# SBUF laid out anew: split weights between the two groups of moving operands, work tiles on the right

## The chip, the cores and the metric

One core of a Trainium2 chip runs the kernel. The metric is the device time of one execution in microseconds (us); lower is better. The program is the same in every execution, so times of three runs and one profiled execution stand for it.

## What is computed

One decoder layer on x of 1024 x 1024 float32: a pooling mixer and a gated convolutional feed-forward network, each behind a root-mean-square norm and with a residual.

```
h = rms_norm(x, norm_mix_g)
# four groups of 256 channels, windows 2, 4, 8, 16:
d = (causal window mean of h) - h
x = x + pool_scale * (d @ pool_w[group] + pool_b)
h = rms_norm(x, norm_ffn_g) @ w_in            # 1024 x 5632
h = causal_depthwise_conv(h, conv_w, conv_b)  # 3 taps
val, gate = split(h)                          # 2816 each
x = x + (silu(gate) * val) @ w_out            # 2816 x 1024
```

## The kernel before, in words

**Stages.** The mixer runs over eight blocks of 128 rows; each block is normed, windowed, multiplied with the pooling weights, added to x (stored to DRAM as x1), normed again and transposed. Then comes the input projection, over 22 pairs of feature blocks (`order`, line 295), and at the end the output projection, over 11 feature pairs.

**Seven products for eight.** Both projections use Strassen's scheme in Winograd's form. A matrix product of 2 x 2 blocks is made of seven block products instead of eight, at the price of sums of blocks. In the input projection the sums of the weights (A11, A12, S1, S2, S3, S4, A22) are made anew for each feature block on VectorE; the sums of the activations (B11, T1, B21, T2, T3, B22, T4) are made once and kept.

**Split operands.** Each operand of a product is split into a high part (float32r, rounded) and a low part, the rest. `split` (line 72) does it for a weight block: ScalarE copies to the high part, VectorE subtracts. `product` (line 339) makes a block product of 12 matmuls of 128x512: for each of four slices of 128 rows, high x high, high x low and low x high. The weights are the stationary operand, the activations (the "nop" tiles) the moving one. In the profile, where numbers at the end of names are left out, "B" stands for B11, B21 and B22 and "T" for T1 to T4; the weight's name beside it tells which, by the table `STEPS`: A11s goes with B11, S2s with T2, S1s with T1, A12s with B21, S3s with T3, S4s with B22, A22s with T4. That is also the order of the products in a round, one round for each n. `event` (line 417) prepares the weights of the product five ahead and issues one product. After it VectorE and ScalarE take the bank's result, and at a round's end `gated` (line 399) makes the convolution, silu and product on VectorE and ScalarE and stores the block to DRAM. X, Y and Z are PSUM banks' tags.

**Output projection.** It loads blocks of the gated activations and of w_out into the nop tiles' places, makes the sums, and splits both operands into "hl" tiles (oAP, oBP), so both the stationary and the moving operand of its matmuls (line 636) are hl tiles.

**Where tiles lie.** SBUF has one address range for each of 128 partitions. Pools are taken from its left end (low addresses) or from its right end (`side="right"`), as stacks. A pool that is closed makes room for the next on its side. Before the change the pools are:

- left, from below: `const`; `nop_a` (B11, T1, B21); `work` (x_edge and later ha; the small sums; the raw weight loads; the seven hl slots; q1); `n2_pool` (n2f, the normed and transposed activations), after it `late` (hb, val, gate, q2), after it `fin` (streams and z);
- right, from the top: `pre` (all of the mixer's setup and blocks), after it `nop_b` (B22, T4, T3, T2) and `right` (r).

In bytes within a partition, as the built programs allocate them:

| tiles | before | after |
|---|---|---|
| B11, T1, B21 (16,384 each) | 17,312 / 33,696 / 50,080 | the same |
| seven hl slots (4,096 each) | 93,088 to 121,760 | 66,464 to 95,136 |
| B22, T4, T3, T2 (16,384 each) | 163,808 / 180,192 / 196,576 / 212,960 to 229,344 | 95,136 / 111,520 / 127,904 / 144,288 to 160,672 |
| r | 159,712 to 163,808 | 160,672 to 164,768 |
| mixer's setup (`pre`) | 159,936 to 229,344 | 95,136 to 164,544 |
| n2f | 125,856 to 158,624 | 165,856 to 198,624 |
| hb, val, gate, q2; later streams and z | 125,856 to 158,624 | 165,856 to 198,624 |
| ha | 66,464 to 70,560 | 198,624 to 202,720 |
| small sums | 70,560 to 76,704 | 202,720 to 208,864 |
| raw weight loads | 76,704 to 93,088 | 208,864 to 225,248 |
| q1 | 121,760 to 125,856 | 225,248 to 229,344 |

In the steady rounds each weight keeps to one hl slot: before, A12s at 93,088, S3s at 97,184, A11s at 101,280, S2s at 105,376, S4s at 109,472, S1s at 113,568, A22s at 117,664; after, the same slots 26,624 lower. Within a nop tile the high part takes the first 8,192 bytes and the low part the rest; each matmul reads 2,048 of them.

Of the kernel before, what the change touches and what calls it, by code (L numbers as in the profile page):

```python
# [7 lines left out]
F32 = mybir.dt.float32  # L8
F32R = mybir.dt.float32r
# [5 lines left out]
P = 128  # L15
S = 1024
D = 1024
F = 2816
NS = S // P
NK = D // P  # L20
# [23 lines left out]
NH = 512  # L44
# [4 lines left out]
def trunk_kernel(ctx: ExitStack, tc: tile.TileContext, x, consts, par, rows, pool_w, w_in, w_out, out):  # L49
# [2 lines left out]
    const = ctx.enter_context(tc.tile_pool(name="const", bufs=1))  # L52
    dram = ctx.enter_context(tc.tile_pool(name="dram", bufs=1, space=bass.MemoryType.DRAM))
    ps_x = ctx.enter_context(tc.tile_pool(name="ps_x", bufs=2, space=PSUM))
    nop_a = ctx.enter_context(tc.tile_pool(name="nop_a", bufs=1))
    work = ctx.enter_context(tc.tile_pool(name="work", bufs=1))
    mid = ExitStack()
    n2_pool = mid.enter_context(tc.tile_pool(name="n2_pool", bufs=1))
    pre = ExitStack()
    pp = pre.enter_context(tc.tile_pool(name="pre", bufs=1, side="right"))  # L60
    ps_p = pre.enter_context(tc.tile_pool(name="ps_p", bufs=3, space=PSUM))

    def bank2(name):
# [3 lines left out]
        return work.tile([P, 2, D], F32, tag="raw", name=name, bufs=2)  # L67

    def hl_tile(name):
        return work.tile([P, 2, NH], F32R, tag="hl", name=name, bufs=7)  # L70

    def split(src, name):
        t = hl_tile(name)
        nc.scalar.activation(t[:, 0, :], src, AF.Copy)  # L74
        nc.vector.tensor_tensor(t[:, 1, :], src, t[:, 0, :].bitcast(F32), ALU.subtract)  # L75
        return t


    xs = {}

    def load_x(j):
        if j < 2 or j >= 2 + XBUFS:
            xs[j] = work.tile([P, D], F32, tag="hl", name=f"x{j}", bufs=7)
        else:
            xs[j] = pp.tile([P, D], F32, tag="x", name=f"x{j}", bufs=XBUFS)
        nc.sync.dma_start(xs[j], x[j * P : (j + 1) * P, :])
# [5 lines left out]
    def affine(t, src, op, fill, base, pattern, step):  # L92
        nc.gpsimd.affine_select(out=t, in_=src, compare_op=op, fill=fill, base=base, pattern=pattern, channel_multiplier=step)
# [26 lines left out]

    keep_warm(12)
    load_x(0)
    nc.sync.dma_start(cst[:, :E0], consts[:, :E0])

    nc.sync.dma_start(x_edge, x.rearrange("(j r) d -> r j d", r=P)[P - HALO :, :, :])
    nc.sync.dma_start(cst[:, E0:], consts[:, E0:])
    load_x(1)
    nc.sync.dma_start(par_sb, par)
    nc.sync.dma_start(scale_b, rows[:1, :].to_broadcast([P, D]))
    for g in range(0, NG, 2):  # L130
        nc.sync.dma_start(wp_raw[:, 2 * g : 2 * g + 4, :], pool_w[g : g + 2].rearrange("g (k p) d -> p (g k) d", p=P))
    for j in range(2, NS):
        load_x(j)
    spread = work.tile([P, NK, P], F32, tag="hl", name="spread", bufs=7)

    eps_t = const.tile([P, 1], F32, tag="eps", name="eps_t")
    nc.vector.memset(eps_t, D * EPS)
# [170 lines left out]
    def tmp(name):  # L308
        return work.tile([P, NH], F32, tag="sum", name=name, bufs=3)
# [30 lines left out]
    def product(bank, a, b, opens):  # L340
        m = 0
        for k in range(4):
            ks = slice(k * P, (k + 1) * P)
            for i, l in ((0, 0), (0, 1), (1, 0)):
                nc.tensor.matmul(bank, a[:, i, ks], b[:, l, k, :], start=opens and m == 0, stop=m == 11, skip_group_check=not opens)  # L345
                m += 1
# [5 lines left out]
    banks, hid = {}, {}  # L352

    def small(tag, name, bufs):
        return work.tile([P, NH], F32, tag=tag, name=name, bufs=bufs)

    def step(n, p):
        a, b, z = STEPS[p]
        opens = p in ("P1", "P6", "P5")
        if opens:  # L360
            pool = ps_x if z == "X" else ps_yz
            banks[n, z] = pool.tile([P, NH], F32, tag=z, name=f"{z}{n}")
        bank = banks[n, z]
        product(bank, aops.pop((n, a)), nops[b], opens)
        tt = nc.vector.tensor_tensor
        if p == "P1":
            hid[n, "q1"] = small("q1", f"q1_{n}", 2)
            nc.scalar.activation(hid[n, "q1"], bank, AF.Copy)
        elif p == "P2":
            hid[n, "a"] = work.tile([P, S], F32, tag="ha", name=f"ha{n}", bufs=1)  # L370
            nc.scalar.activation(hid[n, "a"][:, :NH], bank, AF.Copy)  # L371
        elif p == "P6":
            hid[n, "q2"] = tmp(f"q2_{n}") if n < 2 else late.tile([P, NH], F32, tag="q2", name=f"q2_{n}", bufs=2)
            tt(hid[n, "q2"], bank, hid[n, "q1"], ALU.add)
            if n < 2:
                tt(hid[n, "a"][:, NH:], banks[n, "Z"], hid[n, "q2"], ALU.add)
        elif p == "P5":
            hid[n, "r"] = right.tile([P, NH], F32, tag="r", name=f"r_{n}", bufs=2)
            tt(hid[n, "r"], bank, hid[n, "q1"], ALU.add)
        elif p == "P7":  # L380
            hid[n, "b"] = late.tile([P, S], F32, tag="hb", name=f"hb{n}", bufs=1)
            tt(hid[n, "b"][:, NH:], bank, hid[n, "r"], ALU.add)
        elif p == "P3":
            if n >= 2:
                tt(hid[n, "a"][:, NH:], bank, hid[n, "q2"], ALU.add)  # L385
        else:
            tt(hid[n, "b"][:, :NH], bank, hid[n, "q1"], ALU.add)  # L387
# [29 lines left out]
    def event(k):  # L417
        if k >= 4:
            prep_event(k + LOOK)
        n, p = events[k]  # L420
        step(n, p)
        if p == "P4":
            gated(n)
# [48 lines left out]
            stat(j + 1)  # L472
            stat(j + 2)
    pre.close()
    nop_b = ctx.enter_context(tc.tile_pool(name="nop_b", bufs=1, side="right"))
    right = ctx.enter_context(tc.tile_pool(name="right", bufs=1, side="right"))
    ps_yz = ctx.enter_context(tc.tile_pool(name="ps_yz", bufs=3, space=PSUM))
    for b in ("T2", "T3", "B22", "T4"):
        nops[b] = nop_tile(nop_b, b)
# [22 lines left out]
        split_n(nops["T4"], t4[:, ks], ks=ks)  # L502
    mid.close()
    late_stack = ExitStack()
    late = late_stack.enter_context(tc.tile_pool(name="late", bufs=1))
    for k in range(9, len(events)):
        event(k)
    late_stack.close()


    fin = ctx.enter_context(tc.tile_pool(name="fin", bufs=1))
    free = []

    def take(name):
# [91 lines left out]
    for k in range(-SLOOK, len(oevents)):  # L606
        p, f = oevents[k + SLOOK] if k + SLOOK < len(oevents) else (None, 0)
# [11 lines left out]
        p, f = oevents[k]  # L619
        set_, opens = chains[p]  # L620
        if f == 0 and opens:
            for i in range(4):
                tag = ("XXYY" if set_ == "X" else "YZZZ")[i]
# [92 lines left out]
```

## Time and profile before

| | |
|---|---|
| median of 3 runs | 714.81 us (714.56 to 716.27) |
| the profiled execution's own time | 715.61 us |
| its span, first to last instruction | 713.9 us |
| mean granted TensorE clock | 0.999 |
| matmuls recorded on TensorE | 3149 |

The profile is of one execution. PE is TensorE's matmuls, PEld its weight loads, DVE is VectorE, ACT ScalarE, POOL GpSimd, SP SyncE, which issues the DMAs. A row of the timeline gives the start of a group of equal instructions, the time from its start to its end, its tiles as out<-in, the shape and the count. A matmul's recorded duration holds its way through the array and overlaps the next one, so how long a matmul or a product holds TensorE is read from one start to the next. The chain that ended last is followed back from the last instruction, at each step to what released it. L345 is line 345 of the kernel before; in the kernel after the lines from 55 on are two further down (L347, and L638 for the output projection).

### The profile page before, as it was taken

How to read it: one execution, taken by the hardware profiler on the slowest of the kernel's cores; microseconds unless marked ns; L12 is line 12 of the kernel's file. 1: busy time of each engine (PE TensorE's matmuls, PEld its weight loads, DVE VectorE, ACT ScalarE, POOL GpSimd, SP SyncE). 2: the span in 40 equal slices, each digit the busy share in tenths (PEclk: the TensorE clock that was granted, in tenths of full speed). 3: DMA queues.
4: the chain of work that ended last, by engine and by line, in shares of the span. 5: the costliest groups of instructions: out<-in, count | busy, mean ns of one | idle time of the engine just before them, and what ended most of it. 6: DMA issues, size and time to landing. Idle time of an engine off the chain costs nothing.

```text
span 713.9 us, 8484 instructions
## 1 busy us (share of the span) xinstructions
PE 701.3 (98%) x3149; PEld 572.5 (80%) x3150; DVE 604.8 (85%) x897; ACT 341.9 (48%) x515; POOL 6.5 (1%) x24
## 2 busy tenths in 40 slices
PE   7999999999999999999999999999999999999997
PEld 5898777888888888888888888888887788888885
DVE  4789999999888888888888888876987997798993
ACT  5696546545444544444544444454443544443441
POOL 3000000000000000000000000000000000000000
PEclk9999999999999999999999999999999999999999
DMA  9622032132221122222222212119988800006241
GB/s 307 252 90 87 7 114 75 72 139 80 78 81 53 73 89 89 90 88 90 89 88 89 85 64 89 62 69 350 314 294 295 306 20 1 1 0 206 90 147 59
DMA packets 31001, 83.37 MB, mean 117 GB/s; under 512 B 3416, under 2 KB 4720, under 8 KB 28144
## 3 DMA queue, kind: packets, MB, share of 16 engines
q1 hardware_dynamic: 30864, 82.82, 32.4%
q8 instruction: 24, 0.39, 0.2%
q14 instruction: 17, 0.14, 0.1%
q0 software_dynamic: 96, 0.02, 0.0%
HBM read 62.89 MB, written 19.92 MB: 116 GB/s over the span
## 4 chain that ended last, share of the span: by engine, by line
PE 82%; DMA 8%; DVE 7%; issue 1%; ACT 1%; SPq 1%; POOL 0%; DVEq 0%; ACTq 0%
PE Y L345 24%; PE oP L636 21%; PE X L345 15%; PE Z L345 15%; DMA blk<-g_dram 4%; PE psy L243 3%; DMA blk<-in_w_out_dram 2%; PE psd L172 2%; DVE T L292 1%; DMA x_edge<-in_x_dram 1%; DVE n2f L303 1%; DMA B21s<-in_w_out_dram 1%; PE pst L272 1%; DMA bias_hl<-rows_raw 1%; DVE oBP L75 1%
## 5 line engine op out<-in xcount | busy, mean ns | idle before, releaser
L636 PE MATMUL oP<-oBP,oAP 128*128 128x512 f32 x924 | 211.7, 390 | 1.4 <-DVE oBP L75 0.9
L636 PEld LDWEIGHTS oP<-oBP,oAP 128*128 128x128 f32 x924 | 173.1, 188 | 39.9 <-DVE oBP L75 2.6
L345 PE MATMUL Z<-T,S1s 128*128 128x512 f32 x264 | 65.0, 394 | 1.5 <-ACT T L291 1.1
L345 PE MATMUL X<-B,A11s 128*128 128x512 f32 x264 | 65.6, 394 | 0.7 <-DVE A11s L75 0.7
L345 PE MATMUL Y<-T,S2s 128*128 128x512 f32 x264 | 65.1, 394 | 0.5 <-DVE T L292 0.4
L345 PE MATMUL Y<-T,S3s 128*128 128x512 f32 x264 | 64.3, 392 | 0.0
L345 PE MATMUL Y<-T,A22s 128*128 128x512 f32 x264 | 64.1, 392 | 0.0
L345 PE MATMUL Z<-B,S4s 128*128 128x512 f32 x264 | 63.9, 391 | 0.0
L345 PE MATMUL X<-B,A12s 128*128 128x512 f32 x264 | 63.6, 390 | 0.0
L345 PEld LDWEIGHTS Z<-T,S1s 128*128 128x128 f32 x264 | 49.3, 188 | 13.6 <-ACT T L291 1.6
L345 PEld LDWEIGHTS Y<-T,S2s 128*128 128x128 f32 x264 | 49.3, 188 | 12.5 <-DVE T L292 0.9
L345 PEld LDWEIGHTS X<-B,A11s 128*128 128x128 f32 x264 | 49.3, 188 | 12.2 <-DVE A11s L75 1.1
L345 PEld LDWEIGHTS Y<-T,S3s 128*128 128x128 f32 x264 | 49.5, 188 | 11.2
L345 PEld LDWEIGHTS Y<-T,A22s 128*128 128x128 f32 x264 | 49.5, 188 | 11.1 <-ACT val L392 0.3
L345 PEld LDWEIGHTS Z<-B,S4s 128*128 128x128 f32 x264 | 49.6, 188 | 10.9
L345 PEld LDWEIGHTS X<-B,A12s 128*128 128x128 f32 x264 | 49.5, 188 | 10.3
L403 ACT ACTIVATE gate<-gate 128x1024 f32<-128x1024 f32 x22 | 23.4, 1062 | 43.2 <-DVE gate L394 43.0
L74 ACT ACTIVATE oBP<-blk 128x512 fp32r<-128x512 f32 x32 | 20.2, 633 | 46.9 <-PE oP L636 41.6
L393 DVE SCALAR_TENSOR_TENSOR val<-ha,par_sb,val 128x1023 f32<-128x1023 f32 x22 | 28.2, 1282 | 12.5 <-ACT val L392 12.5
L385 DVE TENSOR_TENSOR ha<-Z,q 128x512 f32<-128x512 f32 x20 | 13.8, 692 | 23.9 <-PE Z L345 23.8
L392 ACT ACTIVATE gate<-hb,par_sb 128x1024 f32<-128x1024 f32 x22 | 27.4, 1245 | 11.9 <-DVE hb L387 11.9
L371 ACT ACTIVATE ha<-X 128x512 f32<-128x512 f32 x22 | 13.2, 600 | 41.2 <-PE X L345 41.2
(129 smaller groups left out, 1020.5 us busy)
## 6 DMA issues: line engine op xcount, KB each, us to landing
win<-in_w_in_dram SPq DMA_DIRECT2D x22, 1024.0 KB, 4.8
g_dram<-val SPq DMA_DIRECT2D x22, 512.0 KB, 2.6
blk<-g_dram SPq DMA_DIRECT2D x33, 256.0 KB, 5.4
blk<-in_w_out_dram SPq DMA_DIRECT2D x31, 256.0 KB, 5.5
A12s<-g_dram SPq DMA_DIRECT2D x22, 256.0 KB, 4.6
B21s<-in_w_out_dram SPq DMA_DIRECT2D x22, 256.0 KB, 2.6
x<-in_x_dram SPq DMA_DIRECT2D x8, 512.0 KB, 9.6
x_dram<-x SPq DMA_DIRECT2D x8, 512.0 KB, 2.6
```

Source lines behind the costliest of these rows:

```text
L74: nc.scalar.activation(t[:, 0, :], src, AF.Copy)
L75: nc.vector.tensor_tensor(t[:, 1, :], src, t[:, 0, :].bitcast(F32), ALU.subtract)
L172: m = nc.tensor.matmul(ps[:, c * P : (c + 1) * P], src[:, c * P : (c + 1) * P], weights[:, c // 2, :], start=True, stop=True)
L243: nc.tensor.matmul(o, dh[:, c, :], wps[:, c, :], start=c % 4 == 0, stop=False, skip_group_check=True)
L272: nc.tensor.transpose(ps[:, c * P : (c + 1) * P], n2[:, c * P : (c + 1) * P], ident)
L345: nc.tensor.matmul(bank, a[:, i, ks], b[:, l, k, :], start=opens and m == 0, stop=m == 11, skip_group_check=not opens)
L371: nc.scalar.activation(hid[n, "a"][:, :NH], bank, AF.Copy)
L385: tt(hid[n, "a"][:, NH:], bank, hid[n, "q2"], ALU.add)
L392: nc.scalar.activation(t, src, AF.Identity, bias=par_sb[:, CB + f : CB + f + 1], scale=w[2])
L393: nc.vector.scalar_tensor_tensor(t[:, 1:], src[:, : S - 1], w[1], t[:, 1:], op0=ALU.mult, op1=ALU.add)
L403: nc.scalar.activation(gate, gate, AF.Silu)
L636: nc.tensor.matmul(obanks[set_, i], a[:, u, i * P : (i + 1) * P], b[:, v, :], start=opens and g == 0 and m == 0, stop=g == NP2 - 1 and m = ...
```

## The change

Some pools change sides and one new pool is made. The hl tiles (split weights, and some x blocks early on) get a pool of their own, `hls`, taken on the left right after `nop_a`. `pre`, and after it `nop_b` and the pool of r, come next on the left. `work`, `n2_pool`, `late` and `fin` go to the right. No instruction is added, removed or moved: each engine has the same instructions in the same order (559 rows of equal instructions on PE, 891 on DVE, 499 on ACT, 16 on POOL, 202 on SP), and each of them waits for the same values of the same semaphores as before. The pool that takes the place of `pre` still waits for it, and the one that takes the place of `n2_pool` for that. What is different in the built program is the addresses in the table above.

```diff
     nop_a = ctx.enter_context(tc.tile_pool(name="nop_a", bufs=1))
-    work = ctx.enter_context(tc.tile_pool(name="work", bufs=1))
+    hls = ctx.enter_context(tc.tile_pool(name="hls", bufs=1))
+    work = ctx.enter_context(tc.tile_pool(name="work", bufs=1, side="right"))
     mid = ExitStack()
-    n2_pool = mid.enter_context(tc.tile_pool(name="n2_pool", bufs=1))
+    n2_pool = mid.enter_context(tc.tile_pool(name="n2_pool", bufs=1, side="right"))
     pre = ExitStack()
-    pp = pre.enter_context(tc.tile_pool(name="pre", bufs=1, side="right"))
+    pp = pre.enter_context(tc.tile_pool(name="pre", bufs=1))
...
     def hl_tile(name):
-        return work.tile([P, 2, NH], F32R, tag="hl", name=name, bufs=7)
+        return hls.tile([P, 2, NH], F32R, tag="hl", name=name, bufs=7)
...
         if j < 2 or j >= 2 + XBUFS:
-            xs[j] = work.tile([P, D], F32, tag="hl", name=f"x{j}", bufs=7)
+            xs[j] = hls.tile([P, D], F32, tag="hl", name=f"x{j}", bufs=7)
...
-    spread = work.tile([P, NK, P], F32, tag="hl", name="spread", bufs=7)
+    spread = hls.tile([P, NK, P], F32, tag="hl", name="spread", bufs=7)
...
         elif p == "P5":
-            hid[n, "r"] = right.tile([P, NH], F32, tag="r", name=f"r_{n}", bufs=2)
+            hid[n, "r"] = left.tile([P, NH], F32, tag="r", name=f"r_{n}", bufs=2)
...
     pre.close()
-    nop_b = ctx.enter_context(tc.tile_pool(name="nop_b", bufs=1, side="right"))
-    right = ctx.enter_context(tc.tile_pool(name="right", bufs=1, side="right"))
+    nop_b = ctx.enter_context(tc.tile_pool(name="nop_b", bufs=1))
+    left = ctx.enter_context(tc.tile_pool(name="left", bufs=1))
...
-    late = late_stack.enter_context(tc.tile_pool(name="late", bufs=1))
+    late = late_stack.enter_context(tc.tile_pool(name="late", bufs=1, side="right"))
...
-    fin = ctx.enter_context(tc.tile_pool(name="fin", bufs=1))
+    fin = ctx.enter_context(tc.tile_pool(name="fin", bufs=1, side="right"))
```

## The prediction

> **What bounds the kernel now.** I read the page first, then busy time by stage, then the timeline of TensorE through one round, then the chain that ended last. On the page TensorE is busy nearly all the time:
>
> ```profile
> PE 701.3 (98%) x3149; PEld 572.5 (80%) x3150; DVE 604.8 (85%) x897; ACT 341.9 (48%) x515; POOL 6.5 (1%) x24
> ```
>
> The stages (columns: stretch, its length, busy time and instructions of TensorE's matmuls, its weight loads, VectorE, ScalarE and GpSimd, then the granted clock, the DMA share and GB/s) tell where TensorE is not the only limit:
>
> ```profile
> 62.00:125.00 63.00, 60.37 (x270) 47.86 (x269) 62.12 (x88) 34.36 (x52) 0.00 (x0) 1.00 0.20 72
> 125.00:490.00 365.00, 365.00 (x1592) 298.55 (x1591) 311.41 (x404) 171.67 (x232) 0.00 (x0) 1.00 0.24 88
> 490.00:560.00 70.00, 68.58 (x296) 54.86 (x295) 58.96 (x91) 32.58 (x53) 0.00 (x0) 1.00 0.93 320
> 560.00:710.00 150.00, 149.50 (x659) 123.25 (x657) 127.68 (x208) 61.03 (x105) 0.00 (x0) 1.00 0.23 80
> ```
>
> Before 125 us VectorE has no slack (62.12 of 63.00). From 125 to 490 us TensorE never stops (365.00 of 365.00) while VectorE has 53.6 us of slack; around 490 to 560 us the DMA engines are 93% busy; the last stretch is TensorE's again. The clock is granted in full in each stage, so a matmul that takes longer than another doesn't do so for its clock.
>
> What a page cannot show is that equal matmuls do not take equal time. Here is one round of the long stage, a feature block of the input projection: seven products of 12 matmuls each, the same instruction with the same shapes. The columns are start, busy time to the end of the last one's pipeline, and the names; the time a product holds TensorE is the next row's start less its own.
>
> ```profile
> 322.84 2.93 PE L345 MATMUL X<-B,A11s 128*128 128x512 f32 x12
> 325.61 2.93 PE L345 MATMUL Y<-T,S2s 128*128 128x512 f32 x12
> 328.38 2.93 PE L345 MATMUL Z<-T,S1s 128*128 128x512 f32 x12
> 331.15 2.88 PE L345 MATMUL X<-B,A12s 128*128 128x512 f32 x12
> 333.87 2.93 PE L345 MATMUL Y<-T,S3s 128*128 128x512 f32 x12
> 336.63 2.91 PE L345 MATMUL Z<-B,S4s 128*128 128x512 f32 x12
> 339.38 2.91 PE L345 MATMUL Y<-T,A22s 128*128 128x512 f32 x12
> 342.12 0.40 PE L345 MATMUL X<-B,A11s 128*128 128x512 f32 x1
> ```
>
> By the weights' names these are the products with B11, T2, T1, B21, T3, B22 and T4. They hold TensorE for 2.77, 2.77, 2.77, 2.72, 2.76, 2.75 and 2.74 us, 19.28 in all. Only B21 with A12s runs at 2.72, or 226.7 ns a matmul. Two more rows show what that is. The first, of the same timeline, is the tail of the product with B11:
>
> ```profile
> 324.93 0.85 PE L345 MATMUL X<-B,A11s 128*128 128x512 f32 x3
> ```
>
> The second is the last long piece of the chain that ended last, the output projection, whose operands on both sides are split tiles (start, length, engine, tile, line, count):
>
> ```profile
> 556.90 152.61 PE oP L636 x671
> ```
>
> The first nine matmuls with B11 take 324.93 - 322.84 = 2.09 us (232 ns each), the last three 325.61 - 324.93 = 0.68 us (226.7 each). So B11 is not slow as such; it starts slow after T4 and settles. In the output projection 671 matmuls take 152.61 us, 227.4 each, small waits included. So 226.7 ns is the pace of every product whose moving operand lies at 17,312 to 121,760 bytes (the first pool of operands and the split tiles), once it has settled. The products with B22 and T4, whose moving operands lie at 163,808 and above, never settle to it: together 342.12 - 336.63 = 5.49 us for 24, 228.8 each. And each time the program goes from that upper group back to the lower one (T4 to B11, T2 to T1) it pays 0.05 us of settling (2.77 less 2.72), while going up (B11 to T2, B21 to T3) costs some 0.02 us (2.77 or 2.76 beside 2.75).
>
> **The change part by part.** *Order and waits.* Every engine has the same instructions in the same order before and after, and each waits for the same counts of the same semaphores. So nothing is queued behind something new, and no cost comes from order. What differs is addresses alone.
>
> *Moving operands, the term that carries the sum.* All seven now lie in two runs that touch the split weights: B11, T1 and B21 where they were, the weights at 66,464 to 95,136, then B22, T4, T3 and T2 from 95,136 to 160,672. Everything else about these matmuls stays. Two differences could have made the upper group slow, and the trace cannot separate them. One is its alignment: each of its tiles begins at 2,016 past a multiple of 2,048 bytes, all lower tiles and all split weights at 928. After the change all seven tiles and all seven weight slots begin at 928. The other is a line in the address range somewhere between 121,760 and 163,808, above which a moving operand is slow. After the change B22 and all but the end of T4 lie below 121,760, where the trace shows the fast pace; T3 and T2 lie in the strip that no row of before covers. In favour of alignment: the four upper tiles, spread over 64 KiB, show the same pace, where a distance would be expected to grade it; B11 settles to the fast pace though it begins 82 KiB below its weights (101,280 less 17,312), while B22 is slow 53 KiB above its own (163,808 less 109,472). So distance itself is out, and I take it that all seven reach 2.72 us.
>
> A round is then 7 x 2.72 = 19.04 us, 0.24 less. How many rounds count? From this row of the timeline on, TensorE runs without a stop:
>
> ```profile
> 122.24 2.93 PE L345 MATMUL Y<-T,S3s 128*128 128x512 f32 x12
> ```
>
> And in the chain that ended last TensorE is left here:
>
> ```profile
> 480.02 2.78 PE Y L345 x12
> 482.82 0.64 ACT oBP L74
> ...
> 487.69 4.77 DMA blk<-g_dram
> ```
>
> From there a store and loads lead the chain up to the output projection's row at 556.90 us above, and they start as much earlier as the stage before them gets there.
>
> (482.82 - 122.24) / 19.28 = 18.7 rounds, x 0.24 = 4.5 us. The last rounds, after 482.82, are shortened too, but DMA covers them: nothing. In the first two blocks, before 122 us, some nine products use the upper group; at most 0.4 us, but VectorE has no slack there, so I take nothing and keep 0.4 as a bound. The output projection has both operands among the split tiles before and after: nothing, with 0.05 us as a bound for the settling at its start. Is there something late next in the long stage? VectorE needs 311.41 us there and gets 360.5: no.
>
> By the Trainium skill (TensorE: Matmul & The Clock Gate, Part 2, the step on LDWEIGHTS) TensorE reads its two operands through two independent ports, and loading weights takes no bandwidth from the running matmul; by that rule where tiles lie would not matter and this sum would be nothing. The rows above, 2.72 against 2.77 us for the same twelve instructions, do not agree with it as it stands.
>
> *Vector and scalar tiles on the right.* The work tiles, the norm's tile and the gated tiles move up, the norm's setup pool down. VectorE's rows for one form at the two ends of the memory (the first with its tiles between 66,464 and 138,144, the second with its gain and its result at 217,056 and above):
>
> ```profile
> L393 DVE SCALAR_TENSOR_TENSOR val<-ha,par_sb,val 128x1023 f32<-128x1023 f32 x22 | 28.2, 1282 | 12.5 <-ACT val L392 12.5
> L257 DVE SCALAR_TENSOR_TENSOR n<-x,st_b,gain_b 128x1024 f32<-128x1024 f32 x8 | 10.3, 1284 | 0.3
> ```
>
> 1282 and 1284 ns: for VectorE the place makes no difference, so these moves cost nothing. If they did cost (or gain) the 2 ns between these rows, in 2 of 1,283, it would be 0.1 us of the 62 that VectorE is the limit for. ScalarE is busy half the time. DMA has the same issues, sizes and queue; I see no row in which its time goes with the place in SBUF.
>
> *The sum.* The profiled execution took 715.61 us, of which 713.9 are its span and 1.7 lie around it. 715.61 - 4.5 = 711.1. The median of the runs, 714.81, lies 0.8 below the profiled one; from it, 710.3. If all bounds fall on the good side, 4.8 (20 rounds) + 0.4 + 0.05 = 5.2 us, 709.6.
>
> **The rivals.** *A line in the address range, with T3 and T2 above it.* For it: the strip is unseen, and the four slow tiles are also the four highest. Against it: the fast and the slow group differ in alignment too. Then B11, B21 and T4 take 2.72, T2 and T1 keep 2.77, T3 keeps 2.76, and B22, now the first after an upper tile, settles at 2.77: 19.23 a round, 0.05 less, x 18.7 = 0.9 us, 713.9. With the line between T3 and T2 only T2 and T1 stay slow: 0.14 a round (19.14), 2.6 us, 712.2.
>
> *Slower: the line cuts T3 in two.* T3 now runs from 127,904 to 144,288, so a line near its start has the first quarter of its high half below and its low half above, and the product alternates high, low, high. Each triple of matmuls that straddles goes up (0.02) and back (0.05); with two such triples 0.14 a round. The decision is whether the line lies between about 128,000 and 132,000. The gain of 0.05 above is then overdrawn by 0.09, x 18.7 = 1.7 us: 716.5. Against it: it needs the line in a tenth of the unseen strip. The same price would arise wherever the settling is set off more often than twice a round.
>
> *The change does nothing: place is not the cause.* The slow products might be slow for their place in the order, for instance for the PSUM bank they write; the new layout would leave that. For it: B21's product adds to X, which no other product of the round does, while T3, B22 and T4 add to Y and Z. Against it: the output projection adds to banks of all three kinds, and nearly all of it runs at the fast pace. Time: 714.8. The rule of the page named above would end here as well.
>
> **How the numbers follow.** I give 0.50 to the forecast, 0.18 to the line below T3, 0.08 to the line below T2, 0.14 to no effect, 0.07 to the slower case, and 0.03 to something I don't see, split evenly. 0.3% of 714.81 is 2.1 us, about what a measurement can tell from no change. Faster than 712.7: the forecast, the line below T2 and half of the rest, 0.59. Slower than 717.0: 1.7 us falls just short of it, but the number of triples that hop is uncertain, so I count most of that case and half of the rest, 0.08. The same: the remaining 0.33. The range reaches from the forecast with all bounds on the good side and a run at the lower end of the three (714.56 beside 714.81), 709.3, up to no change with that spread, 715.2; outside it stay the slower case and what I don't see. The forecast's own range is 709.4 to 711.4.
>
> **What would show it.** In the profile after: all seven products of a round hold TensorE for 2.72 us, mean durations of their matmul groups alike; a round is 19.04 us; the span is 709.4; DVE, ACT and DMA groups keep their means. The first nine matmuls with B11 are as fast as the last three. If T2 and T3 alone stay at 2.76 or 2.77 the line is right; if T3 is above 2.80 it is cut; if the seven keep their seven times, place was not the cause. The forecast is wrong if rounds get shorter and the time doesn't, which would put a limit that I took as moving along (the DMA stretch to 557 us) at a fixed time.

## The result, and the profile after

| | before | after |
|---|---|---|
| median of four runs each, taken side by side | 714.68 us (714.1 to 716.27) | 709.31 us (707.95 to 709.69) |
| ratio, 95% interval | | 0.9928 [0.9914, 0.9943] |
| the profiled execution | 715.61 us | 709.09 us |
| its span | 713.9 us | 707.4 us |

The kernel is 0.72% faster, 5.4 us by the medians. The forecast was 710.3 us, faster. The page's first row and the row of the VectorE group that the prediction used, of the kernel after:

```profile
PE 695.7 (98%) x3150; PEld 572.6 (81%) x3150; DVE 604.6 (85%) x897; ACT 341.9 (48%) x515; POOL 6.5 (1%) x24
L395 DVE SCALAR_TENSOR_TENSOR val<-ha,par_sb,val 128x1023 f32<-128x1023 f32 x22 | 28.2, 1282 | 12.5 <-ACT val L394 11.8
```

TensorE's busy time fell from 701.3 to 695.7 us. VectorE's (604.8, now 604.6) and ScalarE's (341.9, the same) did not move, and the VectorE group still takes 1282 ns though its tiles lie at the other end of the memory. Now the stages, by windows that follow the work as it got earlier:

```profile
62.00:125.00 63.00, 60.24 (x271) 47.96 (x271) 62.12 (x88) 34.38 (x51) 0.00 (x0) 1.00 0.19 73
125.00:485.00 360.00, 360.00 (x1590) 298.10 (x1589) 310.90 (x404) 171.65 (x232) 0.00 (x0) 1.00 0.24 89
485.00:555.00 70.00, 69.53 (x304) 56.56 (x303) 60.90 (x93) 33.49 (x54) 0.00 (x0) 1.00 0.94 326
555.00:705.00 150.00, 147.96 (x652) 121.96 (x650) 126.27 (x206) 60.22 (x103) 0.00 (x0) 1.00 0.23 79
```

The long stage is still TensorE's alone, and it does 1590 matmuls in 360.00 us where it did 1592 in 365.00: nearly the same work in 5 us less, at the same full clock. Where that lies is seen in one round of the timeline, beside the round in the prediction:

```profile
323.01 2.88 PE L347 MATMUL Y<-T,S2s 128*128 128x512 f32 x12
325.73 2.88 PE L347 MATMUL Z<-T,S1s 128*128 128x512 f32 x12
328.45 2.88 PE L347 MATMUL X<-B,A12s 128*128 128x512 f32 x12
331.17 2.88 PE L347 MATMUL Y<-T,S3s 128*128 128x512 f32 x12
333.89 2.88 PE L347 MATMUL Z<-B,S4s 128*128 128x512 f32 x12
336.61 2.88 PE L347 MATMUL Y<-T,A22s 128*128 128x512 f32 x12
339.33 2.88 PE L347 MATMUL X<-B,A11s 128*128 128x512 f32 x12
342.05 2.88 PE L347 MATMUL Y<-T,S2s 128*128 128x512 f32 x12
```

From each start to the next it is 2.72 us, for all seven products; the round is 342.05 - 323.01 = 19.04 us, where it was 19.28. Last, the chain that ended last, where it leaves TensorE for the loads and where it comes back to it:

```profile
475.49 2.73 PE Y L347 x12
478.25 0.64 ACT oBP L76
...
486.57 5.42 DMA blk<-in_w_out_dram
...
543.46 5.37 DMA B21s<-in_w_out_dram
...
550.35 152.62 PE oP L638 x671
```

The chain leaves TensorE at 478.25 instead of 482.82, which is 4.57 us earlier, and reaches the long row of the output projection at 550.35 instead of 556.90, 6.55 earlier. That row is as long as before (152.62 and 152.61). So 4.6 us had been gained by the time the chain leaves the rounds, and in this pair of executions another 2.0 us came from the stretch of loads between.

### The profile page after: what moved, and what is told of

Same layout as the page of the kernel before. It is cut to its first block, busy times and chain, and to the rows that moved or that the text cites. A ratio compares the mean times of both kernels' runs of the same rounds, so it can differ in the third digit from the quotient of the medians.

```text
span 707.4 us, 8485 instructions
## 1 busy us (share of the span) xinstructions
PE 695.7 (98%) x3150; PEld 572.6 (81%) x3150; DVE 604.6 (85%) x897; ACT 341.9 (48%) x515; POOL 6.5 (1%) x24
## 4 chain that ended last, share of the span: by engine, by line
PE 82%; DMA 8%; DVE 6%; ACT 1%; issue 1%; SPq 1%; POOL 0%; DVEq 0%; ACTq 0%
PE Y L347 24%; PE oP L638 22%; PE X L347 15%; PE Z L347 15%; PE psy L245 3%; DMA blk<-g_dram 3%; DMA blk<-in_w_out_dram 2%; PE psd L174 2%; DVE T L294 1%; DMA x_edge<-in_x_dram 1%; DVE n2f L305 1%; DMA B21s<-in_w_out_dram 1%; PE pst L274 1%; DMA g_dram<-val 1%; DMA bias_hl<-rows_raw 1%
## 5 line engine op out<-in xcount | busy, mean ns | idle before, releaser
L76 ACT ACTIVATE oBP<-blk 128x512 fp32r<-128x512 f32 x32 | 20.2, 632 | 46.7 <-PE oP L638 41.3
L395 DVE SCALAR_TENSOR_TENSOR val<-ha,par_sb,val 128x1023 f32<-128x1023 f32 x22 | 28.2, 1282 | 12.5 <-ACT val L394 11.8
```

The costliest lines, as they stand in the source:

```text
L395: nc.vector.scalar_tensor_tensor(t[:, 1:], src[:, : S - 1], w[1], t[:, 1:], op0=ALU.mult, op1=ALU.add)
```

## The experiments

Two stories were open. *Alignment*: it matters where an operand lies within some block of bytes. *Region*: it matters in what part of the memory it lies. A third, that the place is not the cause, fell with the timeline above, since nothing but places was changed. The following kernels put unused bytes ahead of a pool and leave every instruction where it was. In all of them the bytes of one partition are meant; "distance" is the address of the moving operand less that of its weights, modulo 256 where that is said. The time that a product holds TensorE is read, as above, from start to start. In the expectations theory 1 is the alignment of the moving operand against its weights, 1b the alignment of a tile by itself, and theory 2 the region. Each ratio is to executions of the kernel before taken side by side with the run (medians from 713.72 to 714.63 us).

**The layout before, with 1,088 bytes of padding on the right.** The upper group stays high, behind all the work tiles, but begins at 928 past a multiple of 2,048, as the weights do.

```diff
+    pad = ctx.enter_context(tc.tile_pool(name="pad", bufs=1, side="right")); pad.tile([P, 272], F32, tag="pad", name="pad")
     pp = pre.enter_context(tc.tile_pool(name="pre", bufs=1, side="right"))
```

> The layout before, with 1,088 unused bytes at the right end, so that B22, T4, T3 and T2 stay far up (162,720 to 228,256) but begin at 928 past a multiple of 2,048 like the weights and B11, T1 and B21. Theory 1 (alignment of moving operand against weights decides): all seven products hold TensorE for 2.72 us, a round is 19.04 us, the time is about 709.5 us, 0.993 of before. Theory 2 (a line in the address range): nothing changes, 2.77, 2.77, 2.77, 2.72, 2.76, 2.75 and 2.74 us, a round of 19.28, 714.7 us.

Measured: 709.55 us (708.59 to 710.74) beside 713.94 for the kernel before, ratio 0.9938 [0.9918, 0.9958]. From T4's product to the one with T2 in its timeline:

```profile
335.69 2.88 PE L345 MATMUL Y<-T,A22s 128*128 128x512 f32 x12
338.42 2.88 PE L345 MATMUL X<-B,A11s 128*128 128x512 f32 x12
341.13 2.88 PE L345 MATMUL Y<-T,S2s 128*128 128x512 f32 x12
343.86 1.52 PE L345 MATMUL Z<-T,S1s 128*128 128x512 f32 x6
```

2.73, 2.71 and 2.73 us: B11 has no settling after T4 any more, and T2 is as fast as the rest. The old layout with padding does what the whole change does, so the region is out.

**The layout after, with the same padding between the weights and the upper group.** The opposite: all tiles where the change puts them, the upper group 1,088 further.

```diff
+    pad = ctx.enter_context(tc.tile_pool(name="pad", bufs=1)); pad.tile([P, 272], F32, tag="pad", name="pad")
     pp = pre.enter_context(tc.tile_pool(name="pre", bufs=1))
```

> The layout after, with 1,088 unused bytes between the split weights and B22, T4, T3 and T2, which stay near (96,224 to 161,760) but begin at 2,016 past a multiple of 2,048 while the weights begin at 928. Theory 1 (alignment against the weights): the seven times of before come back, a round of 19.28 us, about 714.5 us. Theory 2 (a line in the address range): as after, 7 times 2.72 us, 709.4 us.

Measured: 714.36 us (713.58 to 715.17), ratio 1.0002 [0.9992, 1.0012]. Its timeline:

```profile
322.81 2.93 PE L347 MATMUL X<-B,A11s 128*128 128x512 f32 x12
325.57 2.93 PE L347 MATMUL Y<-T,S2s 128*128 128x512 f32 x12
...
339.34 2.91 PE L347 MATMUL Y<-T,A22s 128*128 128x512 f32 x12
342.08 2.93 PE L347 MATMUL X<-B,A11s 128*128 128x512 f32 x12
```

B11 holds TensorE for 2.76 us again, T4 for 2.74, and the round is 342.08 - 322.81 = 19.27: the whole gain is gone, with the new layout in place. Alignment, then. But alignment of what? The next two kernels ask whether it is that of each operand by itself.

**The layout after, with everything shifted.** The padding goes ahead of the first pool, so that the lower tiles, the weights and the upper tiles all begin at 2,016 past a multiple of 2,048, where the upper group was slow before.

```diff
+    pad = ctx.enter_context(tc.tile_pool(name="pad", bufs=1)); pad.tile([P, 272], F32, tag="pad", name="pad")
     nop_a = ctx.enter_context(tc.tile_pool(name="nop_a", bufs=1))
```

> The layout after, with 1,088 unused bytes below B11: every moving operand and every split weight begins at 2,016 past a multiple of 2,048. Theory 1 (moving operand against weights): nothing changes from after, 7 times 2.72 us, 709.4 us. Theory 1b (a tile's own alignment): all seven products at 2.75 us, 228.8 ns a matmul, and the output projection too, 2 us more there: about 716 us. Theory 2 (a line): as after.

Measured: 709.43 us (708.92 to 710.03), ratio 0.9933 [0.9914, 0.9953]. First and last row of a round:

```profile
323.00 2.88 PE L347 MATMUL Y<-T,S2s 128*128 128x512 f32 x12
...
342.04 2.88 PE L347 MATMUL Y<-T,S2s 128*128 128x512 f32 x12
```

19.04 us, all fast. So 2,016 is as good a place as 928, if the weights lie there too.

**The layout after, with the padding ahead of the weights.** Now the weights and the upper tiles are at 2,016, and the lower tiles stay at 928.

```diff
+    pad = ctx.enter_context(tc.tile_pool(name="pad", bufs=1)); pad.tile([P, 272], F32, tag="pad", name="pad")
     hls = ctx.enter_context(tc.tile_pool(name="hls", bufs=1))
```

> The layout after, with 1,088 unused bytes between B21 and the split weights: weights, B22, T4, T3 and T2 begin at 2,016 past a multiple of 2,048, B11, T1 and B21 at 928. Theory 1 (alignment of the moving operand against the weights): now the three products with B11, T1 and B21 never settle (2.75 us and more), and the four others do, after 0.02 to 0.05 us where they follow one of the three; a round of some 19.2 to 19.3 us, about 714 us. Theory 1b (alignment of the moving operand alone, whatever the weights): as in the layout with the pad behind the weights, B22, T4, T3 and T2 slow, B21 at 2.72 us. Theory 2 (a line): 7 times 2.72 us, 709.4 us.

Measured: 715.2 us (714.01 to 716.13), ratio 1.0012 [1.0, 1.0024]. Its timeline:

```profile
322.65 2.96 PE L347 MATMUL X<-B,A11s 128*128 128x512 f32 x12
325.45 2.90 PE L347 MATMUL Y<-T,S2s 128*128 128x512 f32 x12
328.19 2.96 PE L347 MATMUL Z<-T,S1s 128*128 128x512 f32 x12
330.99 2.96 PE L347 MATMUL X<-B,A12s 128*128 128x512 f32 x12
333.79 2.90 PE L347 MATMUL Y<-T,S3s 128*128 128x512 f32 x12
336.53 2.88 PE L347 MATMUL Z<-B,S4s 128*128 128x512 f32 x12
339.25 2.88 PE L347 MATMUL Y<-T,A22s 128*128 128x512 f32 x12
```

The slowness has changed sides. B21 (with A12s), the one product that was fast before, holds TensorE for 333.79 - 330.99 = 2.80 us, as B11 does (2.80); B22, which never settled before, takes 2.72. T2 and T3, the first after a slow one, take 2.74. What counts is the distance between the moving tiles and the split weights, and the place of either counts for nothing.

Two kinds of access touch a slot of split weights in these rounds: ScalarE and VectorE make the splits in it (L76 and L77), and TensorE's weight loads read it. The moving tiles are only read. If the splits were what slows the matmuls, only matmuls beside a split would be slow. The rows of this kernel during the product with B11 (322.65 to 325.45 above; the second row is the same product from its fifth matmul on):

```profile
322.85 0.63 ACT L76 ACTIVATE A22s<-win 128x512 fp32r<-128x512 f32 x1 [0.70 <-PE Y L347]
323.58 1.79 PE L347 MATMUL X<-B,A11s 128*128 128x512 f32 x7
325.18 0.69 DVE L77 TENSOR_TENSOR A22s<-win,A22s 128x512 fp32r<-128x512 f32 x1
```

ScalarE works on the split until 323.48 and VectorE from 325.18 on. The first four matmuls take 323.58 - 322.65 = 0.93 us (232 ns each), the eight others, nearly all without a split beside them, 325.45 - 323.58 = 1.87 us (234 each). So the splits are not it. What is left of the accesses to these slots is the weight loads; that is by elimination, not by a run that changes the loads.

**How far the distance reaches: two sizes of padding.** The kernel with padding ahead of `pp`, with 64 and with 256 bytes in place of 1,088 (which is 4 x 256 + 64). Their expectations speak of two scans: these are the first two kernels of the next part, which ran before them.

```diff
-    pad.tile([P, 272], F32, tag="pad", name="pad")
+    pad.tile([P, 16], F32, tag="pad", name="pad")
```

> The layout after, with 64 unused bytes between the split weights and B22, T4, T3 and T2. If only the distance modulo 256 bytes counts, as the two scans say, these 64 bytes do what 1,088 did: 2.77, 2.77, 2.77, 2.72, 2.76, 2.75 and 2.74 us, a round of 19.28 us, about 714.4 us. If the large offset or the crossing of some larger boundary counted, 64 bytes do nothing: 7 times 2.72 us, 709.4 us.

> As the other one, with 256 unused bytes. A period of 256 bytes: 7 times 2.72 us, a round of 19.04 us, 709.4 us. A period of 512 or more: B22, T4, T3 and T2 slow, about 714 us.

Measured: with 64 bytes 714.6 us (713.9 to 715.2), ratio 0.9998 [0.9987, 1.0009]; with 256 bytes 709.75 us (709.36 to 710.03), ratio 0.9931 [0.9915, 0.9948]. The round with 64 bytes:

```profile
322.76 2.93 PE L347 MATMUL X<-B,A11s 128*128 128x512 f32 x12
...
342.04 2.93 PE L347 MATMUL X<-B,A11s 128*128 128x512 f32 x12
```

and with 256 bytes:

```profile
322.76 2.88 PE L347 MATMUL Y<-T,S2s 128*128 128x512 f32 x12
...
341.80 2.88 PE L347 MATMUL Y<-T,S2s 128*128 128x512 f32 x12
```

19.28 us, the round of the kernel before to the hundredth, and 19.04. Sixty-four bytes of padding bring back all that the change gained; 256 cost nothing.

**A distance for each product.** Three kernels give each moving tile a pool of its own in the layout after, with gaps between the pools, so that one round shows seven distances. TensorE has one longer wait in them ahead of the long stage (1.3 us beside 0.2 in the kernel after), so their rounds tell more than their total times. The first:

```diff
+LOW = (("B11", 0), ("T1", 256), ("B21", 512)); GAP = 0; HIGH = (("B22", 32), ("T4", 32), ("T3", 64), ("T2", 128))
...
-    nop_a = ctx.enter_context(tc.tile_pool(name="nop_a", bufs=1))
+    for b, n in LOW: nop_pool(b, n)
...
-    nop_b = ctx.enter_context(tc.tile_pool(name="nop_b", bufs=1))
+    for b, n in HIGH: nop_pool(b, n)
```

> The layout after, with a pool of its own for each moving tile and gaps between them, so that each begins at another distance from its weights, in bytes modulo 2,048: B21 0, B22 32, T4 64, T3 128, T2 256, T1 -512, B11 -768. Theory 1 with the weights' and operands' slices of 512 bytes as the period: B21 and T1 hold TensorE for 2.72 us once settled, all others for 2.74 to 2.80, T4 as before (2.75). Theory 1 with a short period, 128 or 256 bytes as banks of the memory would give: T3 or T2, and B11, are fast too. Theory 1 with a period of 2,048: T1 is slow too. If 226.7 ns a matmul is itself the cost of a bad distance, one of them is faster than 2.72, down to 12 x 216 ns = 2.59 us, which float32 and bfloat16 matmuls of the trace take.

Measured: 713.72 us (713.12 to 715.62), ratio 1.0 [0.9986, 1.0014]. Its timeline:

```profile
325.19 2.88 PE L355 MATMUL Y<-T,S2s 128*128 128x512 f32 x12
327.91 2.88 PE L355 MATMUL Z<-T,S1s 128*128 128x512 f32 x12
330.63 2.88 PE L355 MATMUL X<-B,A12s 128*128 128x512 f32 x12
333.35 2.95 PE L355 MATMUL Y<-T,S3s 128*128 128x512 f32 x12
336.14 2.96 PE L355 MATMUL Z<-B,S4s 128*128 128x512 f32 x12
338.94 2.92 PE L355 MATMUL Y<-T,A22s 128*128 128x512 f32 x12
341.70 2.91 PE L355 MATMUL X<-B,A11s 128*128 128x512 f32 x12
```

T2 lies 256 bytes off, T1 512 (below), B21 at 0: each 2.72. T3 at 128 takes 2.79, B22 at 32 takes 2.80, T4 at 64 takes 2.76. (B11, 768 below, is 0 modulo 256 too; it takes 2.75 in the chain that ended last, as the first one after T4.) The second kernel has the gaps 0, 32, 64 below the weights, 32 ahead of them, and 96, 64, 32, 128 above:

> As the other scan, with the distances B11 -128, T1 -96, B21 -32, B22 96, T4 160, T3 192 and T2 320 bytes. Period of 512: all seven are slow, 2.74 to 2.80 us, a round of 19.3 us or more, over 714 us. Period of 128: B11 is fast, the others are not. Sign matters, as with 1,088 and -1,088 bytes (2.75 and 2.80 us): the three below the weights are the slowest. Any product under 2.72 us would show a better distance than 0.

Measured: 720.04 us (719.65 to 720.42), ratio 1.0081 [1.0052, 1.0111], the slowest layout of all. Every product is off, and none takes under 2.76 us:

```profile
326.29 2.95 PE L355 MATMUL X<-B,A11s 128*128 128x512 f32 x12
329.07 2.92 PE L355 MATMUL Y<-T,S2s 128*128 128x512 f32 x12
331.83 2.97 PE L355 MATMUL Z<-T,S1s 128*128 128x512 f32 x12
...
345.83 1.55 PE L355 MATMUL X<-B,A11s 128*128 128x512 f32 x6
```

The round is 345.83 - 326.29 = 19.54 us, 0.50 over the aligned one. T2, at 320 bytes, takes 329.07 to 331.83, 2.76, like T4 at 64 in the kernel ahead of it, which is the period of 256 once more. The sign adds nothing: T1, 96 below its weights, and T4, 160 above, agree modulo 256, and both take 2.81 in the chain that ended last. The third kernel asks for distances under 32 bytes, by views that begin 4 to 24 bytes into their tiles. These tiles are 32 bytes longer, and gaps of 224 make that up to 256; B11 and T1 stay at 0:

```diff
+OFF = {'B22': 4, 'T4': 8, 'T3': 16, 'T2': 24, 'B21': 12}
...
+        o = OFF.get(name, 0) // 4
+        t = nop_pools[name].tile([P, 8 * NH + 8 * (o > 0)], F32R, tag="nop", name=name, bufs=1)
+        return t[:, o : o + 8 * NH].rearrange("p (l k s) -> p l k s", l=2, k=4)
```

> As the two scans, with distances that are no multiples of 32 bytes, modulo 256: B22 4, T4 8, T3 16, T2 24, B21 12; B11 and T1 0. If the memory is read in lines of 32 bytes or more and the distance counts in whole lines, all seven settle at 2.72 us. If every byte counts, the five are slower than 2.72 us, up to the 2.80 that 32 bytes gave. If 0 is not the best distance but near it, one of them is faster than 2.72 us, and a kernel with that distance for all would beat both.

Measured: 717.51 us (717.0 to 717.68), ratio 1.0038 [1.0022, 1.0054]. The worst product of all runs is the one that is off by a single number of 4 bytes, B22 with S4s:

```profile
338.74 3.00 PE L357 MATMUL Z<-B,S4s 128*128 128x512 f32 x12
341.58 2.95 PE L357 MATMUL Y<-T,A22s 128*128 128x512 f32 x12
```

2.84 us, 237 ns a matmul. The idea that blocks of 32 bytes were what had to agree falls with this row. What the runs gave, by distance modulo 256, for 12 matmuls (the first of them still settle, so a row says little under 0.03 us):

| distance mod 256 | us | from |
|---|---|---|
| 0 | 2.72 | all seven products of the kernel after |
| 4, 8, 12 | 2.84, 2.79, 2.75 | B22, T4, B21 of the third kernel |
| 16, 24 | 2.77, 2.81 | T3, T2 of the third |
| 32 | 2.80 | B22 of the first |
| 64 | 2.74 to 2.76 | B22, T4 before; T4 of the first; T2 of the second |
| 96 | 2.80 | B22 of the second |
| 128 | 2.79, 2.78 | T3 of the first, B11 of the second |
| 160 | 2.81, 2.81 | T4, T1 of the second |
| 192 | 2.80, 2.79 | B11 and B21 with the weights shifted; T3 of the second |
| 224 | 2.80 | B21 of the second |

Nothing is faster than 0, 64 is the mildest of the multiples of 32, and there is no slope with the distance.

## Why the prediction was right, and where it was not

*Order and waits cost nothing.* Right: the kernel before with padding alone takes 709.55 us and the kernel after 709.31, so the new sides themselves brought nothing that these runs can tell.

*All seven products reach 2.72 us, a round 19.04.* Right to the hundredth, in the change and in the padded kernel before.

*The cause.* Half right. The prediction chose alignment over a line in the address range, and the pair of padded kernels bears that out: far and aligned is fast, near and not aligned is slow. But it tied the slow pace to the upper tiles' own place (2,016 past a multiple of 2,048, where all else is at 928) without saying whether that counts by itself or against the weights, and it said that "distance itself is out" since B11 was fast 82 KiB from its weights and B22 slow at 53 KiB. That step failed. The distance is what counts, only not its size: its remainder by 256. B11's distance before, 101,280 - 17,312 = 83,968, is 328 x 256; B22's, 163,808 - 109,472 = 54,336, is 212 x 256 + 64. Both rows were in the prediction. The forecast came out right in spite of this, and to that extent by luck: the change puts every tile at 928 and so makes all distances agree as well. For the kernel with everything shifted the two part: a tile's own alignment would make it slow (about 716 us by the expectation), and 709.43 was measured.

*4.5 us from 18.7 rounds.* Right. By the chain it is 4.57 us, of which 0.08 was there when the long stage began (the row at 122.24 starts at 122.16 now) and 4.49 came from its rounds. So the two blocks ahead of it, put at nothing with 0.4 as a bound, gave 0.08. *The rounds after it are covered by loads: nothing.* Nearly right: the last matmul of the input projection starts 4.71 us earlier (491.42, was 496.13 in the traces), 0.14 more. What the forecast had not is the rest, 6.55 - 4.71 = 1.84 us between there and 550.35. What TensorE's weight loads wait for in that stretch, of the kernel before and of the one after (columns: us in total, times, longest):

```profile
PEld oP L636 <- DVE oBP L75: 2.2, 4, 0.6
PEld oP L636 <- ACT oBP L74: 1.7, 3, 0.9
```

```profile
PEld oP L638 <- DVE oBP L77: 1.1, 2, 0.5
PEld oP L638 <- ACT oBP L76: 0.7, 2, 0.4
```

3.9 us of waits became 1.8: splits of loaded weights that came too late for TensorE four or three times, and now twice each. Whether the change did that stays open. From the last matmul of the input projection to the start of the long row there are 254 matmuls in every profile. What that stretch takes beyond 254 x 226.67 ns is 3.2 us before and 1.4 after; 1.2 to 2.1 in the four kernels with every distance at 0, 2.0 to 3.2 in the four with a distance of 64 or 192, and 1.6 to 2.2 in the three kernels with seven distances, which are slow too. The groups overlap, and one profile of each doesn't settle it. By the medians, the three padded kernels with every distance at 0 are 4.4 to 4.9 us under the kernel before and the change is 5.4. So the 4.6 us that the traces show by the end of the rounds agree with all four, and up to 0.8 us beside them stay without a shown cause. The forecast, 710.3, was 1.0 us above the measured median. (The upper end of its range, no change with a spread of 0.25 us, comes to 715.1 and not 715.2; nothing hangs on it.)

*VectorE, ScalarE and DMA.* Right, by the rows above; the 62.12 us that VectorE is busy from 62 to 125 us are 62.12 again.

*The rivals.* The line in the address range, in all three places, fell with the padded kernel before: its upper group lies as high as ever. Nothing was cut in T3 (2.72). The rival by which addresses are not the cause fell with every run. Here the Trainium skill (TensorE: Matmul & The Clock Gate, Part 2, the step on LDWEIGHTS), by which a weight load uses a port of its own and takes nothing from the matmul that runs, does not agree with this trace as it stands: with the two operands 64 bytes apart modulo 256, the same instructions take 0.9% longer (228.8 beside 226.7 ns), and at 4 bytes 4% longer. The recorded weight loads themselves take 188 ns on average before and after. That the weight load and the moving read meet somewhere in the memory would fit all rows, but no run here shows it directly; one would need a kernel in which the weights are loaded once and many matmuls use them, and that wasn't tried. Nor do the runs tell whether a matmul's own weights count or those loaded for the next one, since the seven slots lie 4,096 bytes apart and so agree modulo 256. Types other than float32r weren't tried.

## What to carry to other kernels

Where TensorE bounds a stage, read the starts of equal matmuls one after the other; products that differ by one per cent for the same instructions may do so for their operands' addresses. For float32r matmuls like these, print the address of each moving and each stationary tile and see that they agree modulo 256 bytes: 64 bytes in front of a pool were enough to lose the whole gain, and a padding (1,088 bytes in the kernel before) got it without a new layout. When two operands are read together, test their difference before you judge either by its own place.

## What the runs showed of the hardware

A float32r matmul of 128 x 512, with a weight load for each, takes 226.7 ns in these rounds when the addresses of its two operands agree modulo 256 bytes, at distances from 12 KiB (B22 after the change) to 104 KiB (T2 in the padded kernel before), whichever side of the weights it lies on; and 228 to 237 ns when they don't; 4 bytes are enough. After a product with another distance the new pace takes some matmuls to set in: before, the first nine with B11 ran at 232 ns, though their own addresses agreed. Read to the nanosecond over the rounds of the long stage, the tenth still takes 231 on average, and the last two 226.5. The mean recorded durations shift by the same few nanoseconds as the starts (389 for B21 and 391 for T4 in the rounds before, 399 for B22 at 4 bytes), but since each of them overlaps the next matmul, only the starts show what it costs.
